# Modulation columns at even distances in the conv tiles: double steps further apart, finished columns spread with the next one

## The chip, the cores and the metric

One Trainium2 chip, one core. The engines are TensorE (PE in the profile; its weight loads are PEld), VectorE (DVE), ScalarE (ACT), GpSimd (POOL) and SyncE (SP), which issues most of the loads. The metric is the device time of one execution in microseconds; the times given are the median of three runs, and one more execution is recorded by the profiler. A difference of about 0.2% (3.6 us) is what can be told from no change.

## The reference

A trunk of two layers on 1024 tokens of 1024 channels. Both layers have the same frame; layer 0 mixes tokens by a gated convolution, layer 1 by pooling over windows:

```python
c_act = jax.nn.silu(c)
for i in range(DEPTH):
    mod = c_act @ ada_w[i] + ada_b[i]
    sh_m, sc_m, g_m, sh_f, sc_f, g_f = jnp.split(mod, N_ADA, axis=-1)
    h = modulate(rms_norm(x, norm_mix_g[i]), sh_m, sc_m)
    y = conformer_conv(...) if i % N_MIXERS == 0 else multiscale_pool(...)
    x = x + (1.0 + g_m)[:, None, :] * y
    h = modulate(rms_norm(x, norm_ffn_g[i]), sh_f, sc_f)
    y = swiglu_ffn(h, ffn_w_gate[i], ffn_w_up[i], ffn_w_down[i])
    x = x + (1.0 + g_f)[:, None, :] * y
return rms_norm(x, final_g)

def conformer_conv(h, w1, b1, w_dw, b_dw, ln_g, ln_b, w2, b2):
    a, g = jnp.split(h @ w1 + b1, 2, axis=-1)
    u = a * jax.nn.sigmoid(g)
    u = depthwise causal conv of u, width 31, + b_dw
    return jax.nn.silu(layer_norm(u, ln_g, ln_b)) @ w2 + b2
```

`mod` is one row of 6 x 1024 numbers a layer: six modulation columns j = 0 to 5 (shift, scale, gate of the mixer; shift, scale, gate of the FFN). Each is the product of one vector with a 1024 x 1024 matrix of its own.

## The kernel before

Channels lie on the 128 partitions (8 tiles), tokens along the free axis, in two chunks of 512: A and B. Everything is float32, and each large product is three matmuls of rounded parts: a weight tile and an activation tile are each split in a high and a low part (`hhi`, `hlo`; weights `w`). A tile of the convolution's input has two units on TensorE, `a` (L130, 24 matmuls of 512 columns: 8 channel tiles by 3) and `g` (24 as well). ACT makes the sigmoid of g (a tile `t`), DVE multiplies it onto a (`u`), and DVE, ACT and POOL share the 31 taps: DVE's are the `ca`, ACT makes a product `pr` that POOL adds into a `pa`. One tile of chunk A has its convolution done on TensorE (`ph`, `pc`, `pz`). Tiles go A first, then the shared ones, then B.

Weights arrive on SP's queue as a raw tile; ACT makes the high part (CAST w) and the negated high part (ACTIVATE w), and POOL issues a DMA that adds the weights onto the latter (L411), which gives the low part. There are 9 weight buffers, 4 raw ones, and 6 PSUM banks that all the units named here take in turn; the banks and buffers are what makes a unit wait for the reader of an earlier one.

The modulation columns j = 2 to 5 of layer 0 are computed by TensorE among these units. `ada_columns` walks 4 columns by 8 channel tiles in 16 double steps: two tiles of 512 KB (`adaw`, a pool of two buffers of its own) are multiplied with c_act into a bank `ada` (8 matmuls in the program's rows, 16 records in the profile), and then the next two loads are issued. When a column is complete, `columns_done` copies its rows out of the bank (ACT, `t<-ada`), spreads them onto the partitions with two small products (`adac`), adds the bias (DVE, `mod<-adac`) and makes gains of it (POOL).

The norm of chunk B (`norm_first`) runs among the first units: squares on ACT, their sum `acc` on DVE, then `var` on TensorE, a root on DVE, and `rstd` on TensorE, which spreads it. Later the LayerNorm of chunk A does the same: `mean` on TensorE, squares, `var`, `rstd`, then silu tiles on ACT, their high parts `vhi` and low parts `vlo`, and the product `y` with w2.

What sets the order: TensorE executes in program order. The program is written by a planner: every 12 matmuls of a unit `pace()` lets pending tasks step, according to modelled clocks of DVE, POOL and ACT. A task says with a word that it yields how long it wants to be left alone, in the model's us of TensorE (`LOAD`) or of DVE (`DELAY`). For the columns task these are "late" (the first double step) and "load" (each later one). DVE, ACT, POOL and SP are ordered by a list scheduler with its own estimates; the program's order only sets priorities there. No estimate is a measured time.

Of the kernel before, what the change touches and what calls it, by code (L numbers as in the profile page):

```python
# [9 lines left out]
F32 = mybir.dt.float32  # L10
# [6 lines left out]
P = 128  # L17
D = 1024
S = 1024
KT = D // P  # L20
# [26 lines left out]
PHTAPS = 29  # L47
PHLEN = 135
OUT_B = 3
LOAD = {"load": 4.8, "late": 20.0, "slow": 18.0, "next": 4.0}  # L50
AHEAD = 4
STRETCH = 1.35
LATER = 300
# [60 lines left out]
def trunk(ctx, tc, xT, c, vec, ada, adan, w1, w2, wgu, wdn, wpl, wph, out):  # L114
# [5 lines left out]
    S_ = Engine(nc.scalar, "S", clock, PRICES["S"], lambda i: order(i))  # L120
# [6 lines left out]
    def matmul(out, lhsT, rhs, start, stop, **kw):  # L127
        n = out.shape[-1]
        clock["PE"] += n / 2400 * (1 if rhs.dtype == F32R else 4) + 0.0025
        last_mm[0] = nc.tensor.matmul(out, lhsT, rhs, start=start, stop=stop, **kw).ins.name  # L130

    def order(ins):

        if behind[0] and last_mm[0] is not None:
            tc.add_manual_dep(ins.ins, last_mm[0], edge, reason="behind the products")
        return ins
# [24 lines left out]
    tmp = ctx.enter_context(tc.tile_pool(name="tmp", bufs=2))  # L161
# [4 lines left out]
    def nm(s):  # L166
        uid[0] += 1
        return f"{s}_{uid[0]}"
# [40 lines left out]
    class Task:  # L209
# [6 lines left out]
        def step(self, e):  # L216
            if e != "V" or self.done or clock["PE"] < self.until and not forced[0]:
                return False
            try:
# [3 lines left out]
                if said == "wait":  # L223
                    return False
                if said in LOAD:
                    self.until = clock["PE"] + LOAD[said]
                elif said is not None:
# [10 lines left out]
    def slot(ch, name, dt=F32R):  # L238

        return slots.tile([P, ch.n], dt, tag=f"s{ch.i}", name=nm(name))  # L240
# [5 lines left out]
    def bank(name):  # L246
        return ps.tile([P, 512], F32, tag="mm", name=nm(name))
# [15 lines left out]
    def temp(n, name="t", bufs=0):  # L263
        t = tmp.tile([P, TMPW], F32, tag=name if bufs else "t", name=nm(name), bufs=bufs or 4)
        return t[:, :n]
# [31 lines left out]
    def V(name, j, n=1):  # L297
        b = _COLS[name] + j
        return vecs[:, b : b + n]
# [13 lines left out]
    def ada_load(src):  # L313
        w = raws.tile([P, D], F32, tag="ada", name=nm("adaw"), bufs=ADA_BUFS)
        sync.dma_start(w, src)
        return w
# [26 lines left out]
    def ada_gains(l, j, k, n, eng):  # L343
        b = (l * 6 + j) * KT + k
        m = mod[:, b : b + n]
        lk = l * KT + k
        if j in (1, 4):
            dst, g = (scale_m, "norm_mix_g") if j == 1 else (scale_f, "norm_ffn_g")
            dst = dst[:, lk : lk + n]
            eng.tensor_scalar(dst, m, 1.0, None, op0=ADD)  # L350
            eng.tensor_tensor(dst, dst, V(g, lk, n), op=MUL)
        elif j in (2, 5):
            dst = (gate_m if j == 2 else gate_f)[:, lk : lk + n]
            eng.tensor_scalar(dst, m, 1.0, None, op0=ADD)
            if j == 2 and l % 2 == 1:
                eng.tensor_tensor(dst, dst, V("pool_ls", k, n), op=MUL)

    Q = D // 4

    def ada_columns(js):  # L360


        todo = [(j, k) for j in js for k in range(KT)]
        src = lambda j, k: adan[k, :, (j - 2) * D : (j - 1) * D]
        ws = [ada_load(src(*t)) for t in todo[:ADA_BUFS]]
        for i, (j, k) in enumerate(todo):
            if i % ADA_BUFS == 0:
                yield "load" if i else "late"
            if k == 0:
                acc = bank("ada")  # L370
            w = ws.pop(0)
            for g in range(4):
                matmul(acc[32 * g : 32 * g + 32, :Q], ccols[:, k, :], w[:, g * Q : g * Q + Q], start=k == 0, stop=k == KT - 1)
            clock["PE"] -= 1.3
            if i % ADA_BUFS == ADA_BUFS - 1:
                ws += [ada_load(src(*t)) for t in todo[i + 1 : i + 1 + ADA_BUFS]]
            if k == KT - 1 and (j == 2 or not held[0]):
                yield from columns_done(j, acc)
            elif k == KT - 1:
                held_back.append((j, acc))  # L380

    held, held_back = [False], []

    def columns_done(j, acc):

        rows = temp(Q)
        S_.copy(rows, acc[:, :Q])
        yield "spread"
        cols = bank("adac")
        for h in range(2):  # L390
            matmul(cols[:, 4 * h : 4 * h + 4], rows[:, h * P : h * P + P], quarters, start=True, stop=True)
        m = mod[:, j * KT : (j + 1) * KT]
        V_.tensor_tensor(m.rearrange("p (q h) -> p q h", h=2), cols[:, :KT].rearrange("p (h q) -> p q h", h=2),
                         V("ada_b", j * KT, KT).rearrange("p (q h) -> p q h", h=2), op=ADD)
        ada_gains(0, j, 0, KT, G_)
        ada_done.add((0, j))
# [41 lines left out]
    def mean_rsqrt(acc, n, keep=False, tag="col1"):  # L438

        count = n // P
        yield "stats"
        b = bank("var")
        for i in range(count):
            matmul(b[:, i : i + 1], acc[:, i * P : (i + 1) * P], ones[:, 0:1], start=True, stop=True)
        v, t = b[:, :count], b[:, 16 : 16 + count]
        V_.tensor_scalar(v, v, EPS, None, op0=ADD)
        col = tmp.tile([P, 16], F32, tag=tag, name=nm("col"), bufs=1)[:, :count]  # L450
        yield from rsqrt(v, col, t)
        yield "spread"
        r = spare_bank("rstd") if "taps_done" in st else bank("rstd")
        for i in range(count):
            matmul(r[:, i * P : (i + 1) * P], col[:, i : i + 1].broadcast_to([P, P]), ident, start=True, stop=True)
        r = r[:, :n]
        if not keep:
            return r
        held = temp(n, "ny", 2)
        S_.copy(held, r)  # L460
        return held
# [58 lines left out]
    def norm(ch, l, ffn, key, keep=False, squares=None):  # L520
        h = [(slot(ch, "hhi"), slot(ch, "hlo")) for _ in range(KT)]
        st[key] = h
        if squares is not None:
            rstd = yield from mean_rsqrt(squares.acc, ch.n, keep)
        else:
            rstd = yield from rms(ch, keep)
        for k in range(KT):
            modulated(ch, l, ffn, h, rstd, k)
            yield
# [5 lines left out]
    def unit(emit, *weights):  # L535
        units.append((weights, emit))
# [743 lines left out]
    acc = temp(A.n, "acc", 2)  # L1280
# [143 lines left out]
    def norm_first():  # L1424
        squares = Squares(B, True)
        for k in range(KT):
            squares.add(k)
            yield
        yield from norm(B, 0, False, ("h", 1), squares=squares)
    unit(lambda take: T.__setitem__("norm_b", Task(norm_first(), True)))  # L1430
    taps(A, *range(FIRST))
# [7 lines left out]
    for p in rest[: len(rest) - HOLD - HOLD_LN]:  # L1439
        conv_in((B, p))  # L1440
        if p < 2:
            unit(lambda take, piece=(ph.conv, ph.back)[p]: piece())
    unit(lambda take: held.__setitem__(0, True))
    unit(lambda take: finish(T["ada", 0]))
    unit(lambda take: finish(*(T["taps", 0, p] for p in range(KT) if p not in PHASED)))
    for p in rest[len(rest) - HOLD - HOLD_LN : len(rest) - HOLD]:
# [145 lines left out]
```

## Time and profile before

| | us |
|---|---|
| median of 3 runs | 1823.05 (1819.60 to 1823.14) |
| the profiled execution | 1831.74 |
| its span | 1830.0 |
| outside the span | 1.74 |
| first a unit to mean on TensorE | 64.1 to 227.6 |
| first y product | 246.95 |

The profile is of one execution. Its groups are rows of one kind: line, engine, operation, output from input (buffer numbers left out), shapes and a count; then busy time and the mean of one, and the idle time of the engine ahead of it with what ended it. In the waits view a row names the engine and what waited, what it waited for, and then the total, the number of times and the longest. In the timeline a row has its start, its length and how many instructions it holds, and in brackets the idle time before it and what ended that; lengths of pipelined matmuls overlap, so a price is taken from start to start. The view by windows gives busy time by engine, the clock granted to TensorE (1.00 is full speed) and the share of time in which the DMA engines were busy.

### The profile page before, as it was taken

How to read it: one execution, taken by the hardware profiler on the slowest of the kernel's cores; microseconds unless marked ns; L12 is line 12 of the kernel's file. 1: busy time of each engine (PE TensorE's matmuls, PEld its weight loads, DVE VectorE, ACT ScalarE, POOL GpSimd, SP SyncE). 2: the span in 40 equal slices, each digit the busy share in tenths (PEclk: the TensorE clock that was granted, in tenths of full speed). 3: DMA queues.
4: the chain of work that ended last, by engine and by line, in shares of the span. 5: the costliest groups of instructions: out<-in, count | busy, mean ns of one | idle time of the engine just before them, and what ended most of it. 6: DMA issues, size and time to landing. Idle time of an engine off the chain costs nothing.

```text
span 1830.0 us, 26248 instructions
## 1 busy us (share of the span) xinstructions
PE 1783.3 (97%) x9748; PEld 1525.4 (83%) x9748; DVE 1302.6 (71%) x2127; ACT 1035.7 (57%) x1606; POOL 569.7 (31%) x626
## 2 busy tenths in 40 slices
PE   9999899999999999999999999999999999999997
PEld 7776677888888887899997878999978789999986
DVE  7678755988775238889977458787694468887845
ACT  4665476776647455555554446555454546555543
POOL 0298622877833211311117122110151211011111
PEclk9999999999999999999999999999999999999998
DMA  9858768888888987976767877655568866655562
GB/s 300 256 149 253 211 165 190 224 229 205 230 206 206 242 223 178 262 215 195 202 170 171 195 170 171 157 128 139 143 159 195 180 160 161 183 141 135 133 143 70
DMA packets 115377, 340.63 MB, mean 186 GB/s; under 512 B 11441, under 2 KB 21809, under 8 KB 115250
## 3 DMA queue, kind: packets, MB, share of 16 engines
q1 hardware_dynamic: 76656, 222.56, 36.5%
q0 software_dynamic: 37440, 115.36, 35.2%
q8 instruction: 76, 1.25, 0.3%
q10 hardware_dynamic: 1154, 1.05, 0.2%
q14 instruction: 51, 0.42, 0.1%
HBM read 334.73 MB, written 4.19 MB: 185 GB/s over the span
## 4 chain that ended last, share of the span: by engine, by line
PE 85%; DVE 6%; DMA 3%; issue 2%; ACT 2%; POOL 2%; SPq 0%; POOLq 0%; DVEq 0%; ACTq 0%
PE gate L130 23%; PE up L130 23%; PE dn L130 22%; PE y L130 5%; PE a L130 3%; PE g L130 3%; PE first L130 2%; DMA w<-in_wdn_dram 1%; DVE t L108 1%; DMA adaw<-in_adan_dram 1%; ACT w L108 1%; DVE x L108 1%; DVE win L108 1%; DMA w<-in_wgu_dram 1%; ACT t L108 1%
## 5 line engine op out<-in xcount | busy, mean ns | idle before, releaser
L130 PE MATMUL dn<-ghi,w 128*128 128x512 f32 (+1 forms) x1440 | 470.1, 389 | 5.4 <-DMA w<-in_wdn_dram 4.0
L108 ACT ACTIVATE w<-raw 128x1024 fp32r<-128x1024 f32 (+1 forms) x260 | 240.9, 927 | 340.1 <-PE dn L130 120.5
L108 ACT CAST w<-raw 128x1024 fp32r<-128x1024 f32 (+1 forms) x390 | 319.9, 823 | 129.5 <-PE up L130 54.5
L108 DVE SCALAR_TENSOR_TENSOR x<-dn,gains,x 128x512 f32<-128x512 f32 (+1 forms) x360 | 263.1, 736 | 85.0 <-PE dn L130 81.9
L130 PEld LDWEIGHTS dn<-ghi,w 128*128 128x128 f32 x1440 | 269.2, 189 | 59.2 <-DMA w<-in_wdn_dram 4.8
L130 PE MATMUL gate<-hhi,w 128*128 128x512 f32 (+1 forms) x1088 | 311.7, 360 | 4.0 <-DMA w<-in_wgu_dram 4.0
L130 PE MATMUL up<-hhi,w 128*128 128x512 f32 (+1 forms) x1088 | 310.1, 358 | 0.0
L130 PE MATMUL dn<-glo,w 128*128 128x512 f32 (+1 forms) x720 | 279.3, 388 | 0.9 <-POOL glo L108 0.9
L108 POOL TENSOR_TENSOR pa<-pa,pr 128x512 f32<-128x512 f32 x169 | 231.7, 1459 | 34.8 <-ACT pr L108 32.0
L130 PEld LDWEIGHTS gate<-hhi,w 128*128 128x128 f32 x1088 | 197.2, 189 | 36.0 <-DMA w<-in_wgu_dram 4.9
L1046 POOL DMA_DIRECT2D w<-in_wgu_dram x80 | 69.6, 870 | 495.2 <-ACT w L108 157.3
L130 PEld LDWEIGHTS up<-hhi,w 128*128 128x128 f32 x1088 | 196.7, 189 | 30.5
L130 PE MATMUL gate<-hlo,w 128*128 128x512 f32 (+1 forms) x544 | 195.5, 359 | 1.4 <-DVE hlo L108 1.4
L130 PE MATMUL up<-hlo,w 128*128 128x512 f32 (+1 forms) x544 | 194.6, 358 | 0.0
L411 POOL DMA_DIRECT2D w<-in_wgu_dram x96 | 86.5, 901 | 321.6 <-ACT w L108 298.3
L108 DVE TENSOR_TENSOR t<-t,up 128x512 f32<-128x512 f32 (+1 forms) x88 | 54.9, 625 | 170.4 <-PE up L130 157.6
L108 DVE SCALAR_TENSOR_TENSOR ca<-u,vecs,ca 128x512 f32<-128x512 f32 x251 | 173.4, 748 | 0.7
L130 PEld LDWEIGHTS dn<-glo,w 128*128 128x128 f32 x720 | 136.2, 189 | 24.0 <-POOL glo L108 1.2
L108 ACT ACTIVATE pr<-u,vecs 128x512 f32<-128x512 f32 x169 | 113.5, 716 | 22.4 <-POOL pa L108 12.7
L130 PEld LDWEIGHTS gate<-hlo,w 128*128 128x128 f32 x544 | 103.1, 189 | 18.1 <-DVE hlo L108 2.3
L108 DVE TENSOR_TENSOR w<-raw,w 128x512 fp32r<-128x512 f32 (+1 forms) x130 | 94.3, 733 | 30.8 <-ACT w L108 27.6
L130 PEld LDWEIGHTS up<-hlo,w 128*128 128x128 f32 x544 | 102.6, 189 | 15.5
(190 smaller groups left out, 3341.6 us busy)
## 6 DMA issues: line engine op xcount, KB each, us to landing
raw<-in_wgu_dram SPq DMA_DIRECT2D x176, 512.0 KB, 5.2
w<-in_wgu_dram POOLq DMA_DIRECT2D x96, 512.0 KB, 8.2
raw<-in_wdn_dram SPq DMA_DIRECT2D x88, 512.0 KB, 5.9
adaw<-in_ada_dram SPq DMA_DIRECT2D x64, 512.0 KB, 6.3
w<-in_wdn_dram POOLq DMA_DIRECT2D x48, 512.0 KB, 8.5
raw<-in_w_dram SPq DMA_DIRECT2D x42, 512.0 KB, 6.0
w<-in_wgu_dram POOLq DMA_DIRECT2D x80, 256.0 KB, 5.7
adaw<-in_adan_dram SPq DMA_DIRECT2D x32, 512.0 KB, 5.1
```

The lines of the kernel that those rows point to most:

```text
L108: self.last = self.order(getattr(self.eng, name)(out, *args, **kw))
L130: last_mm[0] = nc.tensor.matmul(out, lhsT, rhs, start=start, stop=stop, **kw).ins.name
L411: order(nc.gpsimd.dma_start(as_src(lo), src, accum_op=ADD))
L1046: order(nc.gpsimd.dma_start(lo, src, accum_op=ADD))
```

## The change

The diff has four parts. The planner's words change: 6.0 instead of 4.8 between double steps, 15 instead of 20 ahead of the first. A new word "settle" (8.0) stands between the squares of chunk B and its norm. A complete column is copied at once into a buffer of its own (`rows`, before one of the four shared `t` buffers), and its two spreading products are written with the next double step, its addition one step on. And the switch `held` goes: before, columns that ended after a given place were kept for the first unit of the output product; now only the last (j = 5) is.

```diff
-LOAD = {"load": 4.8, "late": 20.0, "slow": 18.0, "next": 4.0}
+LOAD = {"load": 6.0, "late": 15.0, "settle": 8.0, "slow": 18.0, "next": 4.0}
...
         ws = [ada_load(src(*t)) for t in todo[:ADA_BUFS]]
+        rows, done = None, iter(())
         for i, (j, k) in enumerate(todo):
             if i % ADA_BUFS == 0:
                 yield "load" if i else "late"
+                next(done, None)
+                if rows is not None:
+                    done, rows = columns_done(j - 1, rows), None
+                    next(done)
             if k == 0:
                 acc = bank("ada")
...
-            if k == KT - 1 and (j == 2 or not held[0]):
-                yield from columns_done(j, acc)
-            elif k == KT - 1:
-                held_back.append((j, acc))
-
-    held, held_back = [False], []
-
-    def columns_done(j, acc):
-
-        rows = temp(Q)
-        S_.copy(rows, acc[:, :Q])
-        yield "spread"
+            if k == KT - 1:
+                rows = tmp.tile([P, Q], F32, tag="rows", name=nm("rows"), bufs=1)
+                S_.copy(rows, acc[:, :Q])
+        held_back.append((j, rows))
+
+    held_back = []
+
+    def columns_done(j, rows):
+
         cols = bank("adac")
         for h in range(2):
             matmul(cols[:, 4 * h : 4 * h + 4], rows[:, h * P : h * P + P], quarters, start=True, stop=True)
+        yield
         m = mod[:, j * KT : (j + 1) * KT]
...
             squares.add(k)
             yield
+        yield "settle"
         yield from norm(B, 0, False, ("h", 1), squares=squares)
...
-    unit(lambda take: held.__setitem__(0, True))
     unit(lambda take: finish(T["ada", 0]))
```

What this does to the order of instructions, at three places (names with their numbers, a tile's number and its allocation; `x4` is four rows of one kind). On TensorE at the norm of chunk B, first the kernel before:

```order
L130 MATMUL g_139_707<-hlo_25_249,w_92_611 128x512
L130 MATMUL g_139_707<-hhi_24_248,w_93_612 128x512
L130 MATMUL var_145_757<-ones_103,acc_118_681 128x1 x4
L130 MATMUL g_139_707<-hhi_26_250,w_92_611 128x512
L130 MATMUL g_139_707<-hlo_27_251,w_92_611 128x512
```

and the changed kernel:

```order
L130 MATMUL g_123_691<-hlo_33_257,w_92_611 128x512
L130 MATMUL g_123_691<-hhi_32_256,w_93_612 128x512
L130 MATMUL var_148_779<-ones_103,acc_118_681 128x1 x4
L130 MATMUL a_158_822<-hhi_18_242,w_103_643 128x512
L130 MATMUL a_158_822<-hlo_19_243,w_103_643 128x512
```

var moved from the middle of the first g unit, 12 matmuls in, to its end; rstd stands 12 matmuls behind var in both. From there on TensorE meets a double step every 36 a or g matmuls in place of every 24.

On ACT around the sigmoid of g_203, the gate unit at which the first of the four columns (j = 2) is completed; before:

```order
L108 ACTIVATE pr_218_1191<-u_98_629,vecs_76 128x512
L108 ACTIVATE pr_219_1195<-u_100_635,vecs_76 128x512
L108 ACTIVATE w_250_1347<-raw_248_1344 128x1024
L108 CAST w_257_1406<-raw_256_1404 128x1024
L108 ACTIVATE t_220_1199<-g_203_1085,vecs_76 128x512
L108 ACTIVATE pr_224_1219<-u_100_635,vecs_76 128x512
```

and now:

```order
L108 ACTIVATE pr_216_1169<-u_98_629,vecs_76 128x512
L108 ACTIVATE w_255_1391<-raw_253_1388 128x1024
L108 CAST w_295_1611<-raw_294_1609 128x1024
L108 ACTIVATE pr_217_1185<-u_100_635,vecs_76 128x512
L108 ACTIVATE pr_218_1189<-u_98_629,vecs_76 128x512
L108 ACTIVATE t_219_1194<-g_203_1085,vecs_76 128x512
L108 ACTIVATE pr_223_1214<-u_100_635,vecs_76 128x512
```

Ahead of the sigmoid stand two weight copies in both; they are of later weight tiles now. w_250 takes the buffer that a_222 reads (before), w_255 the one that g_222 reads with its last but one matmul (now); the next a unit on TensorE is a_246 before, one unit and two double steps behind a_222, and a_244 now, directly behind g_222.

On TensorE between the LayerNorm's rstd and the product y, before:

```order
L130 MATMUL g_387_2140<-hhi_125_689,w_363_2005 128x512
L130 MATMUL rstd_394_2212<-ident_107,col_393_2188 128x128 x4
L130 MATMUL adac_420_2275<-quarters_129,t_391_2168 128x4 x2
L130 MATMUL g_387_2140<-hhi_127_691,w_362_2004 128x512
L130 MATMUL g_387_2140<-hlo_128_692,w_362_2004 128x512
```

(12 more matmuls of g_387 in all, then y) and now:

```order
L130 MATMUL g_386_2130<-hhi_146_777,w_359_1985 128x512
L130 MATMUL rstd_394_2216<-ident_107,col_393_2192 128x128 x4
L130 MATMUL ada_364_2008<-adaw_390_2182,ccols_128 32x256 x4
L130 MATMUL ada_364_2008<-adaw_391_2184,ccols_128 32x256 x4
L130 MATMUL y_428_2306<-vhi_396_2223,w_382_2122 128x512
```

The last double step moved behind rstd, directly ahead of y, and the 12 matmuls that stood there moved ahead of rstd; the spread of the last column (adac) moved behind the first pair of y tiles. ACT copies the last column's rows between the first and the second silu tile (before: ahead of both), and the two weight copies that stood behind the second silu tile stand ahead of the first. The order has 250 conv taps on DVE (251 before) and 170 on ACT and POOL (169 before). Ahead of the first difference at var, and from the first pair of y tiles on, the orders are the same.

## The prediction

> **What bounds the kernel now.** I read the page first, for the engine that is nearly always busy.
>
> ```profile
> span 1830.0 us, 26248 instructions
> PE 1783.3 (97%) x9748; PEld 1525.4 (83%) x9748; DVE 1302.6 (71%) x2127; ACT 1035.7 (57%) x1606; POOL 569.7 (31%) x626
> PE 85%; DVE 6%; DMA 3%; issue 2%; ACT 2%; POOL 2%; SPq 0%; POOLq 0%; DVEq 0%; ACTq 0%
> ```
>
> TensorE (PE) is busy 97% of the span and carries 85% of the chain that ended last, so the change can win only where PE stands still or is clocked down. PE's idle time is about 47 us in all. The instruction orders of the two kernels differ only between about 64 us (the first conv unit behind the "first" tiles) and 261 us (the end of the first pair of y tiles). So I asked for the engines' waits in 60 to 250 us, and for the busy time of the stretch that ends with mean:
>
> ```profile
> PE ada L130 <- DMA adaw<-in_adan_dram: 7.8, 4, 3.9
> PE var L130 <- DVE acc L108: 4.2, 1, 4.2
> PE adac L130 <- ACT t L108: 2.1, 1, 2.1
> PE mean L130 <- DVE acc L108: 1.2, 1, 1.2
> DVE mod L108 <- PE adac L130: 14.2, 3, 7.1
> ACT t L108 <- PE ada L130: 16.4, 2, 8.5
> POOL pa L108 <- ACT pr L108: 21.8, 5, 8.5
> 62.00:228.00 166.00, 150.65 (x859) 113.58 (x858) 128.64 (x198) 103.18 (x146) 122.91 (x120) 0.94 0.71 203
> ```
>
> The columns of the waits are total, times, longest; of the last row: stretch, its length, busy PE, PEld, DVE, ACT, POOL, granted clock, DMA share, GB/s. PE was idle 166 - 150.65 = 15.35 us, and three of its four kinds of wait belong to the modulation columns or to var. A clock of 0.94 over 166 us means another 166 x 0.06 = 10.0 us lost (9 to 11 by the rounding). The timeline of PE shows where that is: behind the waits.
>
> ```profile
> 76.71 1.87 PE L130 MATMUL var<-ones,acc 128*128 128x1 f32 x8 [4.19 <-DVE acc L108]
> 79.43 1.05 PE L130 MATMUL g<-hhi,w 128*128 128x512 f32 x2
> 84.35 0.48 PE L130 MATMUL a<-hhi,w 128*128 128x512 f32 x1
> 85.59 0.62 PE L130 MATMUL a<-hhi,w 128*128 128x512 f32 x2
> 95.44 1.07 PE L130 MATMUL ada<-adaw,ccols 128*32 128x256 f32 x16
> 124.46 1.01 PE L130 MATMUL adac<-quarters,t 128*128 128x4 f32 x4 [2.13 <-ACT t L108]
> 125.33 0.77 PE L130 MATMUL a<-hhi,w 128*128 128x512 f32 x1
> 131.31 0.63 PE L130 MATMUL a<-hhi,w 128*128 128x512 f32 x2
> 143.64 0.64 PE L130 MATMUL ada<-adaw,ccols 128*32 128x256 f32 x8 [2.59 <-DMA adaw<-in_adan_dram]
> 144.21 0.50 PE L130 MATMUL a<-hhi,w 128*128 128x512 f32 x1
> 148.19 0.40 PE L130 MATMUL a<-hlo,w 128*128 128x512 f32 x1
> 191.61 0.64 PE L130 MATMUL ada<-adaw,ccols 128*32 128x256 f32 x8 [3.88 <-DMA adaw<-in_adan_dram]
> 227.63 1.10 PE L130 MATMUL mean<-acc,ones 128*128 128x512 f32 x2 [1.20 <-DVE acc L108]
> 230.24 0.63 PE L130 MATMUL g<-hhi,w 128*128 128x512 f32 x2
> ```
>
> A row's first numbers are start and length. A pair of g matmuls takes 1.05 us behind the wait of 4.19, against 0.62 at 85.59. The 48 a and g matmuls from 84.35 to 95.44 give the full-rate price: 11.09 / 48 = 0.231 us each, 2.8 us for 12. From 125.33 to 131.31 there are 17 in 5.98 us, where 3.9 would do: 2.1 lost, with adac itself (0.87 us, against 0.36 in rows further down) 2.6. From 144.21 to 148.19 it is 10 in 3.98, 1.7 lost. Behind the 1.20 us before mean the pair takes 0.63: no loss.
>
> **The change part by part.** The ceiling: if every one of these stalls went, mean would start 15.35 + 10.0 = 25.3 us earlier. Against that:
>
> *Distance of the double steps.* PE's order has a double step (two 512 KB loads, 16 ada records, 1.0 us) every 24 a/g matmuls before, every 36 now. Its loads leave when the step before has read its two buffers.
>
> ```profile
> adaw<-in_adan_dram SPq DMA_DIRECT2D x32, 512.0 KB, 5.1
> ```
>
> 24 matmuls are 5.5 us, against a median landing of 5.1: hence the four waits. The worst took 5.5 + 3.88 = 9.4 us from step to step; 36 matmuls give 8.3. So even that load would leave 1.1 us, and the median none. Three such steps would be 3.3 us, none is 0; I take 0.5, since the median is nearer. The same spacing puts 13 double steps ahead of mean (14 before) and 12 more matmuls there (480, before 468): 2.8 - 1.0 = 1.8 us lost at mean. I come to what stands behind mean below.
>
> *var later.* It waits for DVE's acc, whose squares ACT makes before anything of the change, so it starts at 76.7 again; now all 24 matmuls of g stand ahead of it and not 12. 4.19 - 2.8 = 1.4 us of waiting stays. Its clock: the nearest row is the 1.20 us before mean (nothing lost), the next the 2.13 (2.6 lost); I take 0 and keep 2.6.
>
> *Spread one step on.* The wait of adac for its copy (2.13) goes, as a step of at least 36 matmuls now lies between copy and use; the 0.4 us of adac itself stays. DVE's mod no longer stands for PE: 14.2 us free.
>
> *A new wait.* In the new order ACT has, ahead of the sigmoid of the second gate unit (t of g_203), the weight copy w_255, which waits for the last but one matmul of g_222; then CAST w_295, pr, pr and that sigmoid. PE's next unit, a_244, needs the bank that this sigmoid reads. So PE can't pass from g_222 to a_244 without a hole. Before, the weight copy ahead of that sigmoid waits for a_222, and g_223 with two double steps stands between that and the next a unit. Prices:
>
> ```profile
> 117.34 1.33 ACT L108 ACTIVATE pr<-u,vecs 128x512 f32<-128x512 f32 x2
> 118.58 0.67 ACT L108 ACTIVATE t<-g,vecs 128x512 f32<-128x512 f32 x1
> 122.14 1.06 ACT L108 ACTIVATE w<-raw 128x1024 fp32r<-128x1024 f32 x1 [0.74 <-PE g L130]
> 123.11 1.03 ACT L108 CAST w<-raw 128x1024 fp32r<-128x1024 f32 x1
> 124.04 0.36 ACT L108 COPY t<-ada 128x256 f32<-128x256 f32 x1
> L411 POOL DMA_DIRECT2D w<-in_wgu_dram x96 | 86.5, 901 | 321.6 <-ACT w L108 298.3
> 164.76 1.28 POOL L108 TENSOR_TENSOR pa<-pa,pr 128x512 f32<-128x512 f32 x1
> ```
>
> By start to start, w 0.97, CAST 0.93, two pr 1.24, t 0.67: 3.8 us, less 0.23 as w_255 starts one matmul early: 3.6. The other way is through POOL: that sigmoid also reuses a buffer which POOL frees one pa behind the DMA issue that w_255 lets go: 0.97 + 0.9 + 1.28 + 0.67 - 0.23 = 3.6, and three hand-overs at about 0.1 (124.46 against the copy's end at 124.40 is 0.06): 3.9. I take 4.0. If both pr wait for a pa of their own it is 4.0 + 2 x (1.28 - 0.62) = 5.3. Clock behind it: 2.6 as behind the 2.13, at least 1.7 as behind the 2.59. So 6.6, between 5.3 and 7.9. Queued behind w_255 on ACT are the pr that feed POOL, and DVE's u waits for the same sigmoid.
>
> [...]
>
> *Behind mean.* Up to rstd the content is the same (48 matmuls and two double steps). Then there were 12 matmuls between rstd and y; now it is the last double step.
>
> ```profile
> 242.88 1.05 PE L130 MATMUL rstd<-ident,col 128*128 128x128 f32 x8
> 243.77 0.51 PE L130 MATMUL adac<-quarters,t 128*128 128x4 f32 x4
> 244.13 0.48 PE L130 MATMUL g<-hhi,w 128*128 128x512 f32 x1
> 246.95 0.39 PE L130 MATMUL y<-vhi,w 128*128 128x512 f32 x1
> 244.75 1.52 ACT L108 ACTIVATE t<-u,vecs 128x512 f32<-128x512 f32 x2 [3.39 <-DVE u L108]
> 246.92 1.07 ACT L108 ACTIVATE w<-raw 128x1024 fp32r<-128x1024 f32 x1
> 248.82 1.51 ACT L108 ACTIVATE t<-u,vecs 128x512 f32<-128x512 f32 x2
> ```
>
> y can't start before the first silu (244.75 + 0.76) and its cast (0.62, an estimate from ACT's other casts of this size): 246.1, at best 0.8 us earlier. The last step's loads leave behind the step ahead of var, 12 matmuls, var and rstd before they are needed (2.8 + 0.8 + 0.9 = 4.5 us): with 5.1 they are 0.6 late, hidden behind the silu; with 9.4 they are 4.9 late and y is late by 4.9 + 1.0 - (246.95 - 243.77) = 2.7. ACT copies its rows between the first two silu, so it would hold the second also. On the other side the two weight operations (246.92 to 248.82, 1.9 us) leave the middle of the silu chain. adac moves behind y: 0.4. I take 0 in sum, between -2.7 (0.8 + 1.9) and +5.7 (2.7 + 0.4, and a clock loss of 2.6).
>
> One conv tap moves from DVE to ACT and POOL (0.62 and 1.28 us there); both have more idle than that in the stretch of 166 us, so I cost it at nothing.
>
> Sum for PE: 25.3 - 1.8 - 1.4 - 6.6 - 0.5 - 0 = 15.0, mean at 212.6. Check against DVE, which sets mean by its last acc: 227.6 less its 14.2 for mod is 213.4. DVE's 128.64 us of work fits (62 + 129 = 191), POOL's 122.91 too. I take the later: a gain of 14. Behind y the orders are the same, so it reaches the end. Profiled execution: 1831.74 (span 1830.0 and 1.74 around it) - 14 = 1817.7. That execution lies 8.7 us above the median of the runs, 1823.05, so the forecast for the median is 1809.
>
> **Rivals.**
>
> *More is won.* The new hole keeps its clock, and DVE, freed of ACT's 16.4 us of standing at the row copies, doesn't hold mean. 25.3 - 1.8 - 1.4 - 4.0 = 18: 1805. For it: the copies' waits came from late double steps. Against: half clock stood behind each of the waits of over 2 us priced above.
>
> *The taps set mean.* PE runs ahead, DVE and POOL don't follow: the 14.2 us come back as waits for sigmoids that stand behind weight copies on ACT. If half comes back, mean is at 213.4 + 7.1 = 220.5: gain 7, 1816. For it: mean waits 1.20 for DVE already, and u waits for that late sigmoid too. Against: POOL's waits for pr, 21.8, came largely while ACT stood at copies.
>
> *The clock stays down.* If the halved matmuls behind 2.13 and 2.59 have a cause of their own, their 2.6 + 1.7 = 4.3 us stay: gain 9.7, 1813. Against: they begin right behind those waits. [...]
>
> *Nothing.* The order moves, but other waits fill the same time: 1823. Against: the adaw waits alone are 7.8.
>
> *Slower.* ACT takes its row copies at fixed places of its order, and waits there for a double step: 16.4 us in two waits before. With PE held at a_244 and steps 36 matmuls apart, the copies of the third and fourth column could come later than ACT stands ready, while POOL starves for pr. If these two waits doubled, to 32.8, the taps and mean would be 16.4 later than 213.4, at 229.8: a loss of 2.2, 1825. It decides from 14 us more on. Against: the steps lose their waits for loads, and the order has the new copies behind more matmuls.
>
> **How the numbers follow.** Forecast 1809 (gains of 11 to 17: 1806 to 1812) 0.50; more 0.15; taps 0.17; clock 0.05; nothing 0.05; slower 0.08. What a measurement of this kernel tells from no change is 0.2%, 3.6 us. Faster by more: 0.50 + 0.15 + 0.05 and most of the taps' 0.17, together 0.86; within: 0.06; slower by more: 0.08, where I keep the whole case and not its middle. The range takes in the better part of both faster rivals: 1802 to 1819, leaving about 0.15 above and 0.04 below.
>
> **What would show it.** No wait of ada for DMA of over 1.1 us, none of adac for ACT; var waiting about 1.4 with full clock behind; a wait of a for ACT's t of about 4, once, with pairs at 1.05 behind it; no long mod wait on DVE; mean at 211 to 215; y starting 18 to 20 us behind mean (19.3 before). The forecast is wrong if ACT's or POOL's chain keeps mean later than 218, or if the last double step holds y by more than 3 us.

## The result, and the profile after

The changed kernel takes 1814.87 us (median of 6 runs, 1809.51 to 1815.43), beside 1820.80 for the kernel before (6 runs, 1819.60 to 1823.14). The ratio is 0.9959, with a 95% interval of 0.9945 to 0.9972. When both were run again it was 1814.30 against 1823.74, ratio 0.9940 (0.9920 to 0.9961). So the change makes the kernel faster: by 6 and 9 us as the medians have it, by 7 and 11 us as the ratios have it. Forecast were 14, and a time of 1809 between 1802 and 1819.

The profiled execution of the changed kernel took 1812.82 us, 18.9 less than that of the kernel before: three times the difference of the medians. Where this comes from is the main question below. First the page of the changed kernel, its head and the chain that ended last:

```profile
span 1811.0 us, 26241 instructions
PE 1774.8 (98%) x9748; PEld 1518.9 (84%) x9748; DVE 1304.9 (72%) x2126; ACT 1037.7 (57%) x1607; POOL 573.0 (32%) x627
PE 87%; DVE 5%; DMA 3%; issue 2%; ACT 2%; POOL 2%; POOLq 0%; ACTq 0%
```

Then its waits in 60 to 250 us, the one row of the window from 62 to 228 us (columns as before: PE, PEld, DVE, ACT, POOL, clock, DMA share, GB/s), and PE's timeline at the places of the prediction:

```profile
PE a L130 <- ACT t L108: 4.3, 1, 4.3
PE ada L130 <- DMA adaw<-in_adan_dram: 2.4, 3, 0.9
PE var L130 <- DVE acc L108: 1.5, 1, 1.5
62.00:228.00 166.00, 159.35 (x939) 120.90 (x938) 141.93 (x222) 115.56 (x164) 129.72 (x126) 0.97 0.78 217
75.40 1.05 PE L130 MATMUL var<-ones,acc 128*128 128x1 f32 x8 [1.49 <-DVE acc L108]
77.74 1.05 PE L130 MATMUL a<-hhi,w 128*128 128x512 f32 x2
133.48 0.79 PE L130 MATMUL a<-hhi,w 128*128 128x512 f32 x1 [4.25 <-ACT t L108]
134.50 1.05 PE L130 MATMUL a<-hhi,w 128*128 128x512 f32 x2
211.69 1.07 PE L130 MATMUL mean<-acc,ones 128*128 128x512 f32 x2
229.85 0.64 PE L130 MATMUL ada<-adaw,ccols 128*32 128x256 f32 x8 [0.81 <-DMA adaw<-in_adan_dram]
231.11 0.64 PE L130 MATMUL ada<-adaw,ccols 128*32 128x256 f32 x8 [0.62 <-DMA adaw<-in_adan_dram]
231.68 0.49 PE L130 MATMUL y<-vhi,w 128*128 128x512 f32 x1
```

The four waits of the kernel before (7.8, 4.2, 2.1, 1.2) are gone or cut to 2.4 and 1.5, and one has come in their place: 4.25 us ahead of a_244, for the sigmoid behind the weight copies, with halved matmuls behind it (pairs of 1.05 us). mean starts at 211.69, before at 227.63.

### The profile page after: what moved, and what is told of

Read it like the earlier page. It is cut to its first block, busy times and chain, and to the rows that moved or that the text cites. A ratio compares the mean times of both kernels' runs of the same rounds, so it can differ in the third digit from the quotient of the medians.

```text
span 1811.0 us, 26241 instructions
## 1 busy us (share of the span) xinstructions
PE 1774.8 (98%) x9748; PEld 1518.9 (84%) x9748; DVE 1304.9 (72%) x2126; ACT 1037.7 (57%) x1607; POOL 573.0 (32%) x627
## 3 DMA queue, kind: packets, MB, share of 16 engines
q8 instruction: 76, 1.25, 0.3%
q10 hardware_dynamic: 1154, 1.05, 0.2%
## 4 chain that ended last, share of the span: by engine, by line
PE 87%; DVE 5%; DMA 3%; issue 2%; ACT 2%; POOL 2%; POOLq 0%; ACTq 0%
PE gate L130 24%; PE up L130 23%; PE dn L130 23%; PE y L130 5%; PE a L130 3%; PE g L130 3%; PE first L130 2%; DMA w<-in_wdn_dram 1%; DVE t L108 1%; DMA adaw<-in_adan_dram 1%; PE ada L130 1%; DVE win L108 1%; DMA w<-in_wgu_dram 1%; DVE x L108 1%; ACT w L108 1%
```

## The experiments

For every kernel the table gives, from PE's timeline of its profiled execution, the time from the first a matmul to mean, from mean to the first y matmul, and from there to the end of the span; then the median of its runs and the ratio to the kernel before as run beside it, with its interval. What is behind the first y takes 1578 to 1584 us in all but one of them, without an order that goes with the kernels; the stage ahead of it makes the difference. Beside the kernels of this table, from top to bottom, the kernel before had medians of 1820.80 (before, changed), 1823.74 (both again, without the hole, 24 matmuls), 1822.59 (the parts alone, no tight place) and 1824.19 us (half loads, without settling). So kernels with different ones beside them are compared by their ratios.

| kernel | a to mean | mean to y | y to end | median | ratio |
|---|---|---|---|---|---|
| before | 163.6 | 19.3 | 1583.0 | 1820.80 | 1 |
| before, again | 159.4 | 19.3 | 1580.6 | 1823.48 | 0.9991 (0.9978 to 1.0004) |
| changed | 148.9 | 20.0 | 1579.3 | 1814.87 | 0.9959 (0.9945 to 0.9972) |
| changed, again | 147.8 | 20.3 | 1583.4 | 1814.30 | 0.9940 (0.9920 to 0.9961) |
| changed, without the hole | 146.6 | 21.0 | 1580.9 | 1814.35 | 0.9945 (0.9925 to 0.9964) |
| changed, 24 matmuls between steps | 167.0 | 21.3 | 1579.2 | 1833.34 | 1.0041 (1.0026 to 1.0056) |
| before, settling alone | 156.1 | 20.6 | 1581.6 | 1821.63 | 0.9992 (0.9979 to 1.0005) |
| before, spread alone | 167.4 | 20.2 | 1580.7 | 1832.65 | 1.0061 (1.0043 to 1.0080) |
| before, distance alone | 156.9 | 37.4 | 1588.0 | 1847.20 | 1.0136 (1.0119 to 1.0153) |
| changed, no tight place | 151.1 | 23.3 | 1583.8 | 1821.00 | 0.9994 (0.9984 to 1.0004) |
| before, half loads | 153.0 | 19.3 | 1579.1 | 1816.19 | 0.9953 (0.9937 to 0.9969) |
| changed with 24, half loads | 160.6 | 21.1 | 1579.6 | 1826.39 | 1.0005 (0.9993 to 1.0017) |
| changed, half loads | 147.4 | 18.3 | 1578.5 | 1811.45 | 0.9924 (0.9910 to 0.9939) |
| changed, without settling | 156.6 | 20.7 | 1580.0 | 1825.38 | 1.0007 (0.9995 to 1.0019) |

### Both kernels a second time

No edit. Two theories stood against each other for the 18.9 us of the profiles beside the 5.9 of the medians.

> The kernel before, unchanged, profiled and timed a second time. The two profiles differ by 18.9 us (1831.74 and 1812.82), the medians by 5.9. Theory 1: the profiled execution of before was a long one inside the stage that the change touches, since its waits for the loads of the double steps (7.8 us and the clock behind them) differ between executions. Then this profile is near 1821, mean starts at 217 to 223 and not at 227.6, and the waits of ada for DMA come to 1 to 4 us. Theory 2: the stage always takes that long and the changed kernel gives the gain back later in most executions. Then mean starts at 226 to 229 again, with 7 to 8 us of waits for those loads, and the difference to 1831.74 lies behind y.

> The changed kernel, unchanged, profiled and timed a second time. Theory 1: its stage hardly depends on the loads, so mean starts at 210 to 214 again, the hole ahead of the second B unit is 4 to 4.5 us, and the time is 1811 to 1816. Theory 2: mean is the same, and what is behind the first y varies by 5 us or more against the first profile (1579.3 us from the first y to the end).

From the second profile of the kernel before, its waits, its window and its timeline behind adac and at mean:

```profile
PE ada L130 <- DMA adaw<-in_adan_dram: 7.3, 6, 3.5
62.00:228.00 166.00, 151.55 (x887) 113.34 (x886) 131.15 (x204) 106.88 (x152) 126.08 (x123) 0.96 0.73 207
123.81 0.61 PE L130 MATMUL adac<-quarters,t 128*128 128x4 f32 x4 [2.13 <-ACT t L108]
124.82 0.62 PE L130 MATMUL a<-hhi,w 128*128 128x512 f32 x2
222.88 1.10 PE L130 MATMUL mean<-acc,ones 128*128 128x512 f32 x2 [0.85 <-DVE acc L108]
242.18 0.39 PE L130 MATMUL y<-vhi,w 128*128 128x512 f32 x1
```

Theory 1 holds in its main point: mean at 222.88, and the stage from the first a to the first y 4.2 us shorter than in the first profile (178.7 against 182.9), of the 7.2 us between the two profiled executions. It was wrong on the waits for loads: they are 7.3 us here too, only cut up in six (the longest but one is 1.25). What differs is the clock. The same wait of 2.13 us ahead of adac was followed by pairs of 1.05 in the first profile and by pairs of 0.62 here; over the window the clock is 0.96 and not 0.94, that is 166 x 0.02 = 3.3 us, and the idle time is 0.9 us less. The changed kernel's stage is steady: 168.9 and 168.1 us. Second against second it is 10.6 us shorter, where the first pair said 14.0. The rest of the 18.9 lies ahead of the first a (1.3) and behind the first y (3.7), where the second pair has the opposite sign (2.8 the other way).

### The hole taken out

Two ACT instructions, the weight copy w_255 and the cast w_295, are ordered behind the sigmoid of g_203; `gates` holds the sigmoids by their number.

```diff
         S_.copy(hi, raw)
+        held = gates.get(219) if uid[0] in (255, 296) else None
...
+        tc.add_manual_dep(S_.last.ins, held, edge, reason="behind the gate")
```

> The changed kernel with two ACT instructions (the weight copy w_255 and the cast w_295) put behind the sigmoid that they stood ahead of; TensorE's order is the same to the last matmul. If the hole of 4.25 us ahead of a_244 is what the prediction says, it goes, with the half clock behind it (about 2.4): mean 6 to 7 us earlier, at 205 to 206, and the whole 5 to 7 us faster than the changed kernel. If DVE or POOL then set mean, it comes at 208 to 211 with a wait for DVE's acc, and 1 to 4 us are won. If the hole was covering another wait, nothing is won.

Its timeline at the hole, at mean and ahead of y:

```profile
132.52 0.50 PE L130 MATMUL a<-hhi,w 128*128 128x512 f32 x1 [2.93 <-ACT t L108]
133.09 0.63 PE L130 MATMUL a<-hhi,w 128*128 128x512 f32 x2
210.40 1.13 PE L130 MATMUL mean<-acc,ones 128*128 128x512 f32 x2 [1.89 <-DVE acc L108]
229.11 0.64 PE L130 MATMUL ada<-adaw,ccols 128*32 128x256 f32 x8 [2.45 <-DMA adaw<-in_adan_dram]
```

The hole shrinks from 4.25 to 2.93, as the sigmoid still stands behind products that POOL paces (ACT's products wait for its additions 29 times up to 232 us, 17.9 us in all), and this time the clock stays full behind it (a pair in 0.63 us). But mean comes only 1.2 us earlier against the first a than in the changed kernel's second profile, and now it waits 1.89 us for DVE. The time is the same (1814.35 against 1814.30). mean to y is 0.7 us longer, with a wait of 2.45 for a load in it. So the hole was real and stood where the prediction put it, but it covered DVE's chain of taps, which ends at most one or two us earlier. In the stage this is the second case of the expectation (mean at 210.40, waiting for DVE); in the time, the third: nothing is won.

### 24 matmuls between the steps again

```diff
-LOAD = {"load": 6.0, "late": 15.0, "settle": 8.0, "slow": 18.0, "next": 4.0}
+LOAD = {"load": 4.8, "late": 15.0, "settle": 8.0, "slow": 18.0, "next": 4.0}
```

> The changed kernel with the planner's word for the distance of the double steps back at 4.8 (24 matmuls between them, not 36); var's later place and the spread one step on stay. If the distance is what removes the waits for loads, they come back: 3 to 8 us of ada waiting for DMA, and the time is 3 to 8 us over the changed kernel's less what the hole ahead of a_244 gives back (its ACT order has no such tight place): between 4 us faster and 4 us slower than the changed kernel. If the spread one step on and var's place carry the gain, the waits for loads stay under 2 us and the time is 5 us under the changed kernel's.

Its waits, PE's first and then DVE's:

```profile
PE ada L130 <- DMA adaw<-in_adan_dram: 12.5, 7, 2.9
PE mean L130 <- DVE acc L108: 7.3, 1, 7.3
DVE u L108 <- ACT t L108: 35.6, 9, 8.8
```

It is slower than expected by either reading: 19 us over the changed kernel and 9.6 over the one before. The waits for loads came back and more (12.5). Besides, DVE stands 35.6 us for sigmoids up to 232 us, where it stood 15.5 in the changed kernel, and mean waits 7.3 for it. Two of DVE's nine waits, 6.77 and 5.50 us long, end with these sigmoids on ACT:

```profile
168.42 1.06 ACT L108 ACTIVATE w<-raw 128x1024 fp32r<-128x1024 f32 x1 [2.67 <-PE g L130]
169.38 0.67 ACT L108 ACTIVATE t<-g,vecs 128x512 f32<-128x512 f32 x1
201.82 0.59 ACT L108 COPY yph<-pc 128x512 f32<-128x512 f32 x1 [6.40 <-PE pc L130]
202.30 0.69 ACT L108 ACTIVATE t<-g,vecs 128x512 f32<-128x512 f32 x1
```

Each stands directly behind an instruction that waits for TensorE, a weight copy and the copy of the convolution done there. So a late TensorE makes these sigmoids late, and with them the taps of DVE, for which mean waits. The other 23 us of DVE's waits are not traced.

### Each part alone on the kernel before

The part `held` has no kernel to itself; it goes in "spread alone" too.

Settling alone:

```diff
-LOAD = {"load": 4.8, "late": 20.0, "slow": 18.0, "next": 4.0}
+LOAD = {"load": 4.8, "late": 20.0, "settle": 8.0, "slow": 18.0, "next": 4.0}
...
+        yield "settle"
         yield from norm(B, 0, False, ("h", 1), squares=squares)
```

> The kernel before with one part of the change, the word ahead of the norm of chunk B: var stands behind all 24 matmuls of the first g unit. If var's wait is worth what the prediction says, it falls from 4.2 to 1.4 us, rstd comes 2.7 us earlier (in the two profiles of before the clock was down behind it both times, for another 3 us), and the whole is 3 to 6 us faster than before. If the taps on DVE and POOL set mean anyhow, mean moves by under 1 us and so does the time.

```profile
PE var L130 <- DVE acc L108: 1.5, 1, 1.5
120.86 0.98 PE L130 MATMUL adac<-quarters,t 128*128 128x4 f32 x4 [6.54 <-ACT t L108]
```

var's wait falls as expected, and the first adac takes it: 6.54 us for its copy, where it was 2.13. mean is 3.3 us earlier than in the second profile of before, y 1.3 us later behind it, and the median doesn't move (0.9992). Neither case of the expectation fits: mean moved and the time did not.

Spread alone: the changed kernel with the planner's words as before and no settling, so the buffer of its own and the switch `held` are as in the changed kernel. The part of it that moves the spread:

```diff
+                next(done, None)
+                if rows is not None:
+                    done, rows = columns_done(j - 1, rows), None
+                    next(done)
```

> The kernel before with the spread of a finished column one step on, and the addition one further on; distances (24 matmuls) and var's place as before. If DVE's 14 us of standing for adac are what holds the taps, mean comes 3 to 8 us earlier. If the waits for the loads hold TensorE, they stay at 7 us or grow, and mean moves by under 2 us. The kernel with 24 matmuls, this spread and var's later place was 9.6 us over before, with mean waiting 7.3 us for DVE: if the spread made that, this one is slower than before by 5 to 12 us.

```profile
PE ada L130 <- DMA adaw<-in_adan_dram: 12.5, 6, 3.6
PE mean L130 <- DVE acc L108: 4.3, 1, 4.3
DVE mod L108 <- PE adac L130: 2.4, 1, 2.4
```

DVE's standing for adac falls from 14.7 to 2.4, and still the kernel is 10 us slower. As no column's spread delays a double step any more, all 16 stand ahead of mean, each 24 matmuls from the next, and their waits for loads grow from 7.3 to 12.5 us. mean waits 4.3 us for DVE besides, so DVE's standing for adac was not all that held the taps.

Distance alone:

```diff
-LOAD = {"load": 4.8, "late": 20.0, "slow": 18.0, "next": 4.0}
+LOAD = {"load": 6.0, "late": 15.0, "slow": 18.0, "next": 4.0}
```

> The kernel before with the two planner's words for the distance alone (36 matmuls, a first step 5 us earlier). The order then has the last three double steps in a row ahead of the LayerNorm's rstd, since each column's spread also takes its time in the row. If the distance carries the gain, the waits for loads ahead of mean fall under 2 us and mean comes 5 to 9 us earlier than in before; but the last two steps behind var each wait a whole landing (about 5 us, so 8 to 10 us), and the time ends 0 to 5 us over before. If the distance does nothing without the rest, mean stays at 222 to 228 and the time is 8 to 10 us over before.

```profile
243.49 1.08 PE L130 MATMUL ada<-adaw,ccols 128*32 128x256 f32 x8 [8.25 <-DMA adaw<-in_adan_dram]
248.33 1.08 PE L130 MATMUL ada<-adaw,ccols 128*32 128x256 f32 x8 [2.10 <-DMA adaw<-in_adan_dram]
252.15 2.08 PE L130 MATMUL rstd<-ident,col 128*128 128x128 f32 x8
257.65 0.79 PE L130 MATMUL y<-vhi,w 128*128 128x512 f32 x1 [3.43 <-DVE vhi L108]
277.07 1.02 PE L130 MATMUL adac<-quarters,t 128*128 128x4 f32 x4 [5.53 <-ACT t L108]
```

mean comes 2.5 us earlier than in the second profile of before, not 5 to 9, and then the three last double steps stand in a row ahead of rstd. The first wait there is 8.25 us, and the rows behind it are at the halved clock, rstd and the first y products too (rstd takes 2.08 us, 1.05 in the first profile of before; the first y matmul 0.79 and 0.39): 37.4 us from mean to y, 18 more than before. Behind the first y the last column's adac waits another 5.53 us for its copy, which is most of the longer rest (1588.0 against 1580.6). The time is 25 us over before, where 0 to 5 or 8 to 10 were expected. The old spread spends words of its own between the steps, so a wider distance pushes the last steps over the edge of the stage; the new spread doesn't.

### No tight place

```diff
-LOAD = {"load": 6.0, "late": 15.0, "settle": 8.0, "slow": 18.0, "next": 4.0}
+LOAD = {"load": 5.6, "late": 13.5, "settle": 8.0, "slow": 18.0, "next": 4.0}
```

> The changed kernel with other numbers for the planner (5.6 between steps, 13.5 ahead of the first): still about 36 matmuls between steps, but no unit waits for a sigmoid that stands behind a weight copy of the unit just ahead, and the last double step stands ahead of rstd, so y follows rstd at once. If the hole was worth its length, mean comes 4 to 6 us earlier than in the changed kernel (211), at 205 to 207. If DVE, ACT and POOL set mean at that point, it comes at 209 to 212 with a wait for DVE's acc of 1 to 4 us. Behind it, y waits about 3 us for its first silu, where the changed kernel waited 1.5 to 2 for loads: y 20 to 22 us behind mean. In sum 1810 to 1816.

```profile
205.70 0.82 PE L130 MATMUL ada<-adaw,ccols 128*32 128x256 f32 x8 [2.90 <-DMA adaw<-in_adan_dram]
215.00 2.05 PE L130 MATMUL mean<-acc,ones 128*128 128x512 f32 x2 [4.15 <-DVE acc L108]
238.28 0.50 PE L130 MATMUL y<-vhi,w 128*128 128x512 f32 x1 [2.15 <-DVE vhi L108]
```

The hole is gone altogether, and the kernel is 7 us slower than the changed one. mean waits 4.15 us for DVE and comes 3.3 us later against the first a; the clock is halved behind that wait (mean takes 2.05 us, 1.10 in the second profile of before), and y is 23.3 us behind mean. Neither place expected for mean (205 to 207, 209 to 212) was met: it is at 215.0. The order was chosen for TensorE's waits alone; the taps end later in it. The profiled execution was the longest of eleven, 2.9 us above their median, so a part of this can be its own. None of the kernels so far beats the changed one.

### Half the loads

```diff
-        sync.dma_start(w, src)
+        sync.dma_start(w[:, : src.shape[-1]], src)
...
-        src = lambda j, k: adan[k, :, (j - 2) * D : (j - 1) * D]
+        src = lambda j, k: adan[k, :, (j - 2) * D : (j - 2) * D + D // 2]
...
-                matmul(..., w[:, g * Q : g * Q + Q], ...)
+                matmul(..., w[:, g % 2 * Q : g % 2 * Q + Q], ...)
```

> The kernel before with the loads of the double steps cut to 256 KB each: every step multiplies the first half of its columns twice, so the columns j = 2 to 5 hold other numbers (left out: the second half of their matrices). The order on TensorE is the same. If the waits of ada for DMA (7.3 and 7.8 us in two profiles, and clock behind them) are what the wider distance removes, they go here without any new order: 0 to 1.5 us of them, mean 5 to 9 us earlier, 6 to 10 us faster. If DVE, ACT and POOL hold mean at that point, mean waits for DVE's acc instead and under 4 us are won.

```profile
PE ada L130 <- DMA adaw<-in_adan_dram: 2.0, 1, 2.0
216.42 1.10 PE L130 MATMUL mean<-acc,ones 128*128 128x512 f32 x2 [1.93 <-DVE acc L108]
```

The kernel before, with nothing new in TensorE's order, gains 0.47% (8.6 us by the ratio) when its loads are halved; mean is 6.4 us earlier against the first a. This is the first case of the expectation, with a wait of 2.0 us left where at most 1.5 was expected. So half the loads' bytes were worth what the change wins on the whole, or nearly. Not all of it need be TensorE's waits: the DMA engines are less busy too (a share of 0.64 in 62 to 228 us, 0.73 in the second profile of before).

> The changed kernel with the same half loads; the second half of the matrices of j = 2 to 5 is left out. Its waits for them are 2.4 to 2.8 us, 1.4 to 1.7 of it right ahead of y. If the wider distance has taken the loads off TensorE's path, only that is won: 1 to 4 us. If the loads still hold ACT or POOL back (their weight copies and low parts share the DMA engines), 5 us or more.

In the changed kernel the same edit is worth about 3 us by the second ratio (0.9924 after 0.9940) and 6 by the first (0.9959). Against its second profile the stage is only 0.4 us shorter up to mean and 2.0 us between mean and y, where its loads came late for the last two steps. Up to mean the changed kernel's TensorE waits only 0.2 us for loads in any case. By the ratios the loads cost 0.0047 before and 0.0016 to 0.0035 now, so the wider distance won about 0.0012 to 0.0031, 2 to 6 us; and between the two kernels with half loads 0.0029 are left, 5.3 us, that don't come from the bulk of the loads. Each ratio is known to about 0.0015 to 0.002 either way, so this split is rough.

> The kernel with var's later place and the spread one step on but 24 matmuls between the double steps (it was 9.6 us over before, with 12.5 us of ada waiting for DMA), with the same half loads; the second half of the matrices of j = 2 to 5 is left out. If the loads hold that kernel, it drops by 12 to 20 us, to 1812 to 1820, with mean near 211 to 216. If it was slow because DVE's u waits for sigmoids behind weight copies (35.6 us there), it stays over 1826 with mean over 224.

```profile
PE mean L130 <- DVE acc L108: 8.8, 1, 8.8
DVE u L108 <- ACT t L108: 23.3, 9, 9.5
```

The kernel with 24 matmuls between the steps drops by 7 us, from 1833 to 1826, between the two readings. Its loads were one part; the other stays: mean waits 8.8 us for DVE, and DVE 23.3 us for sigmoids. Which instructions ahead of the sigmoids on ACT make that difference against the changed kernel is not traced to single ones in this kernel.

### Without the settling

```diff
-        yield "settle"
```

> The changed kernel without the word ahead of the norm of chunk B: var stands again behind 12 matmuls of the first g unit, and the double steps keep their distance of 36 from there. With var's wait at 4.2 us again and the clock down behind it, TensorE is 3 to 6 us later at rstd; another tight place stands at the last A-side unit (g behind a, one row apart) in place of the hole. If that is what the settling is worth, the time is 3 to 7 us over the changed kernel, still under before. If mean is set by the taps, whose start doesn't hang on var, it is within 2 us of the changed kernel; alone on the kernel before the word was worth nothing (ratio 0.9992).

```profile
PE var L130 <- DVE acc L108: 4.2, 1, 4.2
PE ada L130 <- DMA adaw<-in_adan_dram: 3.9, 2, 2.2
PE g L130 <- ACT t L108: 2.4, 1, 2.4
```

These are waits up to mean. All of the gain is gone: 1825.38, ratio 1.0007, more than the 3 to 7 us that were expected. The way to mean is 8.8 us longer than in the changed kernel's second profile. TensorE's waits make 5.6 of it: 2.8 more for var, 3.7 more for loads (3.9 against 0.2 up to mean), 2.4 at the new tight place and 1.6 ahead of mean, less the hole's 4.25 and 0.6 ahead of rstd, which this order doesn't have. The clock behind var makes 2.8: var to rstd takes 6.7 us at half clock here, and 3.9 in the changed kernel without the wait of 0.6, with 12 matmuls between in both. Together that is 8.4. The word that is worth nothing alone is worth 9 to 12 us among the others, by the ratios; it also moves the double steps behind it, so this is the worth of the order that it leads to, not of var's place only.

## Why the prediction was right or wrong

*The range held the time*, 1814.87 in 1802 to 1819, and the direction was right. The size was not: 6 to 11 us won, by medians and ratios, and 14 forecast.

*The change part by part, against its own execution.* Here the working came out closely. var's wait: 1.4 forecast, 1.49 measured. The hole ahead of a_244: 4.0 forecast, 4.25 measured, in both profiles, with the clock down behind it. mean: 212.6 to 213.4 forecast, 211.69 measured. y behind mean: 18 to 20 forecast, 20.0. adac no longer waits; no wait for a load is over 1.1. DVE's waits for sigmoids up to 232 us were 14.3 and 10.4 in the two profiles of before and 15.5 in both of the changed kernel; they grew, but mean did not wait for DVE. The first a to the first y became 14.0 us shorter in the first pair of profiles, the very number. That is in part luck. Behind var the prediction put the clock loss at nothing, and in the first profile pairs took 1.05 there: the 12 matmuls behind var took 4.4 us, and 3.0 in the second profile. The 12 matmuls behind the hole take 2.8 us at full rate; they took 5.4 and 4.4, so the clock cost 2.6 there, as forecast, and 1.6.

*The step that failed* is the ceiling: "if every one of these stalls went, mean would start 15.35 + 10.0 = 25.3 us earlier", and then the sum taken off the median as it stood. That stall time was one execution's. In the second profile of the same kernel it is 166 - 151.55 = 14.45 us of idle time and 166 x 0.04 = 6.6 us of clock, 21.1 in all, 4.2 less, just what its stage is shorter by. With that TensorE's sum is 15.0 - 4.2 = 10.8; DVE's end, 222.88 - 14.7 = 208.2, is then the earlier bound, so the gain is 10.8 and the time 1812.2. The second pair of stages differs by 10.6 us, and the medians measured were 1814.9 and 1814.3. Two profiles show that the stall time differs between executions; how it is spread over many is not shown. The text noted that the profiled execution lay 8.7 us above the median, but the changed kernel's gain was not made smaller for it. Since the stalls are what the change removes, what an execution has too much of them the change seems to win too.

*The clock behind short waits* was the term at fault inside it. The prediction took 2.6 us behind a wait of 2.13 as a price. It also counted 17 matmuls from 125.33 to 131.31 where the rows hold 14, so the price in that profile was 2.7, and 3.3 with adac; by this the sum for PE would have been 14.3, and the forecast of 14 the same. But it is not a fixed price: the wait of 2.13 ahead of adac was followed by the half clock in one of three profiles (before, before again, before with half loads). The prediction's rows also left out one loss: behind the wait of 3.88 the convolution on TensorE (`pc`) took 9.0 us, and 7.3 in the changed kernel. With it the rows come to 3.1 behind var, 3.3, 1.7 and 1.7, together 9.8 of the 10.0. The rival that the clock stays down forecast 1813, nearer to the measured time than 1809, but its mechanism was not the case: the loss comes and goes between executions of one kernel.

*Rivals.* "More is won" assumed that the hole keeps its clock and DVE doesn't hold mean. In the kernel without the hole the first condition was met (2.93 us, full clock behind it), the second failed: mean waited 1.89 us for DVE, and nothing was won. The check against DVE's own end (213.4), of which the prediction took the later, was the right second bound: the two chains end within one or two us of each other. "The taps set mean" forecast 1816, nearer too, but by a mean at 220.5 that did not come (211.69, with no wait for DVE); only that the taps are next in line came true. "Nothing" and "slower" did not come; but the slower time that the prediction gave to waits at row copies came about in two kernels with one part alone, in another way (loads too close together, steps in a row at the end).

*The parts do not add up.* The prediction priced them within the combined order and forecast none alone, so its prices are good for that order only: settling alone 0.9992, spread alone (with `held` gone) 1.0061, distance alone 1.0136, all together 0.9940 to 0.9959. Each frees a wait that another part's absence puts back: the wider distance needs the spread that doesn't push the steps, the spread needs the distance so that the loads keep up, and without the settling the order behind var is another one.

## What to carry to other kernels

Price a removed stall by what it is in several executions, not in the one that was profiled; where the profiled execution lies well above the median and the stalls in question are waits for transfers with clock behind them, the surplus is in part likely in those rows (here 4.2 of the 7.2 us between two executions). When a planner's numbers change together, read the new order for loops in which an engine waits for an instruction that waits for that engine's last instruction but one: their length can be added up from rows to a few tenths of a us. But removing such a hole wins only down to the next chain, so work that one's end out beside it.

## What the runs showed of the hardware that was not expected

Whether the clock falls behind a short wait is not decided by the wait's length alone. Rows of three profiles: the changed kernel with half loads, the changed kernel's second profile, and "spread alone", two rows each.

```profile
133.42 0.73 PE L130 MATMUL a<-hhi,w 128*128 128x512 f32 x1 [3.05 <-ACT t L108]
134.37 1.05 PE L130 MATMUL a<-hhi,w 128*128 128x512 f32 x2
75.83 1.05 PE L130 MATMUL var<-ones,acc 128*128 128x1 f32 x8 [1.44 <-DVE acc L108]
77.98 0.62 PE L130 MATMUL a<-hhi,w 128*128 128x512 f32 x2
216.09 0.64 PE L130 MATMUL ada<-adaw,ccols 128*32 128x256 f32 x8 [3.56 <-DMA adaw<-in_adan_dram]
218.11 0.62 PE L130 MATMUL a<-hhi,w 128*128 128x512 f32 x2
```

Pairs were halved behind 3.05 (1.05 us), and stayed at full speed behind 1.44 and even behind 3.56 (0.62), as behind the 2.93 and the 2.13 of the rows shown above. Behind 1.49 us the changed kernel's pairs took 1.05 at 77.74 in its first profile; of the eight profiles in which var waited 1.44 to 1.73 us it was the only one. Every wait of 4 us or more in the stage was followed by halved matmuls, 14 in all, from 4.15 to 8.85 us. Waits of one length did one thing in one execution and another in the next: 2.13 us ahead of adac was followed by the half clock in the first profile of before and not in the second. No run here moves a single such wait, so the cause is not shown.
